# A hybrid attention and convolution layer: half of the conv gate by Strassen, adaLN columns moved, norm1's operands in pieces, norm2's statistics one unit later

## The chip, the cores and the metric

One core of one Trainium2 chip runs the kernel. The metric is the device time of one execution in microseconds (us), as the median of several runs. TensorE is called PE, VectorE DVE, ScalarE ACT, GpSimd POOL; SP is the queue from which the transfers here are issued.

## The reference

One layer of an encoder, 1024 prompt tokens and 32 sample tokens (T = 1056 columns), width 1024, all in float32:

```python
mod = (jax.nn.silu(c) @ w_ada + b_ada).reshape(B, 6, 1, D_MODEL)
shift1, scale1, gate1, shift2, scale2, gate2 = [mod[:, i] for i in range(6)]
h = _rms_norm(x, norm1_g) * (1 + scale1) + shift1
q, k, v, xin, gb, gc, ga_br, gb_br = jnp.split(h @ w_in, IN_SPLITS, axis=-1)
...
y_a = o.reshape(B, T, ATTN_DIM) @ w_attn_out          # o: differential attention of q, k, v
u = gc * xin
cv, conv_tail = _short_conv(u, conv_prev, conv_w)     # three taps along time
y_b = (gb * cv) @ w_conv_out
m = jax.nn.sigmoid(ga_br) * y_a + jax.nn.sigmoid(gb_br) * y_b
x = x + gate1 * (m @ w_out)
h2 = _rms_norm(x, norm2_g) * (1 + scale2) + shift2
g, up = jnp.split(h2 @ w_gate_up, 2, axis=-1)
x = x + gate2 * ((jax.nn.silu(g) * up) @ w_down)
```

## The kernel before

Channels lie on the 128 partitions, tokens on the free axis. A float32 operand is split into a high part (an ACT cast) and a low part (a DVE subtraction, L83 to L85), and a product is three matmuls: high by high, high by low, low by high. There are two forms. The classical one takes a column chunk of 128 output channels in three groups of 352 tokens: 8 tiles of the input width, 3 products, 3 groups, 72 matmuls of 352 columns (L1047 to L1049 in the attention, L1075 to L1077 after it). The Strassen form (`wstrassen`, `strassen`, matmul at L181) takes a pair of chunks at once: seven products instead of eight, on quarters of 264 tokens in two groups g of two quarters each, 7 × 2 × 12 = 168 matmuls of 264 columns. Its combining adds are DVE's (L188 to L197).

The stages follow each other. **Start**: columns of `w_ada` are loaded (`ada_load`) and multiplied (`ada_matmul`, `ada_close`, L330 to L345), x is normalised and transposed (`x_norm`, `x_transpose`), modulated (`modulate`), and its Strassen operands are formed (`h_operands(j, g)`, on DVE and ACT, four j by two groups). **Conv loop**: for pairs p = 0, 2, 4, 6 a Strassen call for xin (section 3 of `w_in`) and one for gc (section 5), the multiply u (L474) and the convolution on DVE (L503, L505), whose result goes to `cv_d` in DRAM. **Gate calls**: eight Strassen calls for sections 6 and 7, and behind each two `ada_step`: one column of the remaining 32 (sections 2, 4, 3, 5) per step, computed on DVE (`ada_dve`: 2 instructions of L354, 14 of L357) and, a step later, summed over partitions by two PE transposes into a PSUM tile called pad (L364) and a DVE reduction (L366). Then the eight tiles of h come back from DRAM (`hA`, L567).

**Attention**: 72 units (8 heads, 9 query tiles) whose order a planner writes out, with priorities and estimated durations. Section 4 of `w_in` (gb, times the convolution's result, into `z_d`) is computed there as `filler`: eight classical chunks, in 192 steps that the planner puts where PE has nothing else; what is left follows the last unit. **Conv projection** (`first_w`, `zt`, the loop over n, L1075 to L1094): the first two column chunks run tile by tile as the eight z tiles come in through two staging buffers and are split; the other six run by token groups, one `ada_step` behind each. **Attention projection**: eight column chunks with an `ada_step` each, and then the steps that are left. **Output projection** with the residual (`out_unit`): the last four chunks by quarters q = 0, 2, 1, 3. The squares of the new x are summed on DVE (L1205), `stat(q)` sums them over partitions on PE (L1213) and takes the power on POOL (L1216), and norm2's operands for the Strassen form of gate and up follow (`spread` L1224, `h2_block` L1230 and L1234). A table `after` says behind which unit (q, i) each of these steps stands. **Gate and up** by Strassen, then **down**.

Each engine works in its own order. Outside the attention a scheduler sets it from the order of the code and its own estimates.

## Time and profile before

| | us |
|---|---|
| median of 3 runs | 2137.67 (2137.27 to 2138.59) |
| the profiled execution | 2132.99 |
| span in its trace | 2131.2 |
| PE busy | 2031.0 |
| DVE busy | 1351.4 |
| ACT busy | 847.1 |
| POOL busy | 364.7 |

The trace counts from the start of the span. A row of the timeline gives the start, the duration, the engine, the line and operation, the tile written and those read, the shape, and in brackets the idle time of the engine before it with what ended it. A line number is that of the kernel before.

### The profile page before, as it was taken

What the parts mean: (1) busy time and instruction counts of PE and PEld (TensorE: products, weight loads), DVE (VectorE), ACT (ScalarE), POOL (GpSimd) and SP (SyncE); (2) the same over time, 40 slices, a digit from 0 to 9 for tenths busy, and PEclk for the clock granted to TensorE, in tenths of its full rate; (3) what the DMA queues carried; (4) which work ended last, traced back from release to release, by engine and by line L of the source; (5) the groups of instructions that cost most, each with busy time, mean ns of one, the idle gap of its engine ahead of it and who ended that gap; (6) DMA issues with size and microseconds to landing.
All of it is one profiled execution on the core that took longest, in us unless ns stands there. A gap on an engine that the chain in (4) does not pass through costs nothing. (4 is left out here: it accounts for less than half of the span.)

```text
span 2131.2 us, 37806 instructions
## 1 busy us (share of the span) xinstructions
PE 2031.0 (95%) x14339; PEld 1976.7 (93%) x14339; DVE 1351.4 (63%) x3096; ACT 847.1 (40%) x2044; POOL 364.7 (17%) x660
## 2 busy tenths in 40 slices
PE   7799999899999999999899989889999999999999
PEld 5799999899999999999899989879999999989998
DVE  4988799967766776677357974685555555432322
ACT  5522233366666666666222213463332332321210
POOL 1023100033333333333000000012112112100000
PEclk8899999999999999999999999999999999999999
DMA  8422254532211221121388625123222222552321
GB/s 251 151 84 90 71 161 135 192 89 60 68 57 56 62 59 54 50 69 48 114 258 250 198 90 170 53 68 122 71 73 89 70 80 79 172 157 65 99 69 57
DMA packets 298960, 224.42 MB, mean 105 GB/s; under 512 B 15617, under 2 KB 281498, under 8 KB 298778
## 3 DMA queue, kind: packets, MB, share of 16 engines
q1 hardware_dynamic: 298778, 222.00, 34.0%
q8 instruction: 113, 1.85, 0.4%
q14 instruction: 69, 0.57, 0.1%
HBM read 162.46 MB, written 59.49 MB: 104 GB/s over the span
## 5 line engine op out<-in xcount | busy, mean ns | idle before, releaser
L84 ACT CAST ws<-st 128x512 fp32r<-128x512 f32 x360 | 217.2, 615 | 564.4 <-PE u L181 172.9
L181 PE MATMUL u<-op,ws 128*128 128x264 f32 x3168 | 397.3, 285 | 7.8 <-ACT op L84 6.5
L181 PEld LDWEIGHTS u<-op,ws 128*128 128x128 f32 x3168 | 392.4, 189 | 8.4 <-ACT op L84 6.7
L85 DVE TENSOR_TENSOR ws<-st,ws 128x512 fp32r<-128x512 f32 (+1 forms) x322 | 222.6, 699 | 195.3 <-ACT ws L84 192.9
L181 PE MATMUL u<-T,ws 128*128 128x264 f32 x1536 | 198.5, 287 | 1.2 <-DVE sg L197 1.2
L181 PEld LDWEIGHTS u<-T,ws 128*128 128x128 f32 x1536 | 193.5, 190 | 1.8 <-DVE sg L197 1.8
L731 PE MATMUL b<-qw,hA 128*128 128x384 f32 x512 | 186.8, 365 | 2.5 <-DVE adred L366 1.2
L732 PE MATMUL b<-qw,hA 128*128 128x384 f32 x512 | 174.2, 340 | 0.6 <-DVE qw L688 0.6
L733 PE MATMUL b<-qw,hA 128*128 128x384 f32 x512 | 173.8, 339 | 0.0
L1431 PE MATMUL u<-ka,ws 128*128 128x352 f32 x480 | 156.8, 327 | 4.6 <-ACT ka L84 2.8
L1432 PE MATMUL u<-ka,ws 128*128 128x352 f32 x480 | 155.6, 324 | 2.3 <-DVE ka L85 2.3
L181 PE MATMUL u<-B,ws 128*128 128x264 f32 x1152 | 152.1, 287 | 4.6 <-ACT B L84 4.6
L1433 PE MATMUL u<-ka,ws 128*128 128x352 f32 x480 | 155.7, 324 | 0.0
L181 PEld LDWEIGHTS u<-B,ws 128*128 128x128 f32 x1152 | 145.6, 190 | 5.3 <-ACT B L84 4.9
L357 DVE SCALAR_TENSOR_TENSOR adacc<-adw,sc,adacc 128x128 f32<-128x128 f32 x448 | 132.8, 350 | 0.6
L879 ACT ACTIVATE p<-S,nmx,rs 128x128 f32<-128x128 f32 (+5 forms) x144 | 113.1, 787 | 50.1 <-DVE nmx L959 17.0
L85 POOL TENSOR_TENSOR ws<-st,ws 128x512 fp32r<-128x512 f32 x38 | 49.8, 1311 | 445.3 <-ACT ws L84 426.1
L731 PEld LDWEIGHTS b<-qw,hA 128*128 128x128 f32 x512 | 97.7, 191 | 6.4 <-issue 2.1
L732 PEld LDWEIGHTS b<-qw,hA 128*128 128x128 f32 x512 | 97.9, 191 | 1.2 <-DVE qw L688 0.9
L733 PEld LDWEIGHTS b<-qw,hA 128*128 128x128 f32 x512 | 97.2, 190 | 0.0
L1431 PEld LDWEIGHTS u<-ka,ws 128*128 128x128 f32 x480 | 90.6, 189 | 5.6 <-ACT ka L84 3.5
L1432 PEld LDWEIGHTS u<-ka,ws 128*128 128x128 f32 x480 | 90.7, 189 | 3.1 <-DVE ka L85 3.1
(277 smaller groups left out, 4379.8 us busy)
## 6 DMA issues: line engine op xcount, KB each, us to landing
adw<-in_w_ada_dram SPq DMA_DIRECT2D x48, 512.0 KB, 4.0
st<-in_w_gate_up_dram SPq DMA_DIRECT2D x44, 512.0 KB, 4.0
st<-in_w_in_dram SPq DMA_DIRECT2D x43, 512.0 KB, 4.3
sa<-a_d SPq DMA_DIRECT2D x22, 528.0 KB, 3.6
a_d<-xa SPq DMA_DIRECT2D x84, 132.0 KB, 1.7
st<-in_w_in_dram SPq DMA_DIRECT2D x42, 256.0 KB, 2.9
st<-in_w_down_dram SPq DMA_DIRECT2D x16, 512.0 KB, 5.0
h_d<-xnT SPq DMA_DIRECT2D x8, 528.0 KB, 4.3
```

Source lines behind the costliest of these rows:

```text
L84: act.copy(hi, src)
L85: (lo_eng or dve).tensor_sub(lo, src, f(hi))
L181: pe.matmul(q[dst], l, t[:, r, j, :], start=first and j == n == 0, stop=j == 3 and n == 2, skip_group_check=not first)
L357: dve.scalar_tensor_tensor(out=acc[:, s_, :], in0=st[:, kt, :], scalar=sc[:, 8 * s_ + kt:8 * s_ + kt + 1], in1=acc[:, s_, :], op0=ALU.mult ...
L731: pe.matmul(pj[:, 0:384], a, qh[:, :, c, :], start=kt == 0, stop=False)
L732: pe.matmul(pj[:, 0:384], a, ql[:, :, c, :], start=False, stop=False)
L733: pe.matmul(pj[:, 0:384], b, qh[:, :, c, :], start=False, stop=kt == KT - 1)
L879: act.activation(p[:n, :u["L"]], u["sv"][m][:n], AF.Exp, bias=u["nmx"][:n, m:m + 1], scale=u["rs_t"][:n, m:m + 1], accum_out=sums[:n, m:m ...
L1431: pe.matmul(pt[:, :gw], wh, ah, start=kt == 0, stop=False)
L1432: pe.matmul(pt[:, :gw], wh, al, start=False, stop=False)
L1433: pe.matmul(pt[:, :gw], wl, ah, start=False, stop=kt == KC - 1)
```

## The change

1. In the conv loop, for p = 0 and p = 2, section 4 is now a Strassen call too (`conv_out`), behind the convolution. Its result is multiplied by the convolution's in place, on DVE for the first quarter of each group and on POOL for the other three, and goes to `z_d`; these two pairs no longer go through `cv_d`. `filler` takes only the chunks n = 4 to 7.
2. The last gate call has no `ada_step` behind it; in the conv projection n = 2 to 5 have two. The steps behind the attention projection's loop are none.
3. At the start `ada_order`'s loads and x's loads are interleaved, and the multiplications by columns of `w_ada` (`ada_two`) stand between x's tiles. `h_operands(j, k)` forms group 0 alone, j = 0 and 1 together, and through a tile `hs`. Group 1 is formed by `h_operands_rest`, in pieces over all four j at once, in place in xnT; a hook takes one piece after each of the seven steps of the first Strassen call, under a PE and DVE order as written.
4. `stat(0)`, `stat(2)` and `stat(1)` stand one unit later.

```diff
+    hs = E.tile([P, 2, T], F32, tag="sg", name="hs", bufs=1)
-    def h_operands(j, g):
+    def h_operands(j, k):
...
+    def h_operands_rest():
+
+        def parts(o, src):
+            split(src, Top[o, 1][:, 0], Top[o, 1][:, 1])
+
+        b11, b12, b21, b22 = (xnT[:, 4 * i:4 * i + 4, q * QW:(q + 1) * QW] for i in (0, 1) for q in (1, 3))
+        parts("B11", b11)
+        dve.tensor_sub(b11, b12, b11)
+        yield
+        parts("T1", b11)
+        yield
...
     for j in range(4):
+        if j > 1:
+            ada_two()
+            ada_two()
+            ada_close()
+        modulate(j)
+        modulate(j + 4)
         if j:
-            for i in range(4):
-                ada_matmul()
-                if 7 + 4 * j + i < len(ada_order):
-                    ada_load(ada_order[7 + 4 * j + i])
-            ada_close()
+            h_operands(0 if j == 1 else j, j + 1)
         if j == 2:
             w0 = wstrassen(win_pair(3, 0))
-        modulate(j)
-        modulate(j + 4)
-        h_operands(j, 0)
-        if j:
-            h_operands(j - 1, 1)
     for n in range(KT):
         sp.dma_start(h_d[n], xnT[:, n, :])
-    h_operands(3, 1)
+    rest = h_operands_rest()
...
+    def conv_out(w, p, z):
+        def epi(i, j, g, src):
+            c0 = (g + 2 * j) * QW
+            zb = z[:, i, c0:c0 + QW]
+            (dve if i == j == 0 else pool).tensor_mul(zb, src, zb)
+            sp.dma_start(z_d[p + i, :, c0:c0 + QW], zb)
+
+        strassen(w, (0, 1), lambda i, j, g: tmp("t"), epi)
+
+    NZ = 4
...
-            conv_in(w0, p, (0,), xin)
+            with tc.manual_schedule(engines={mybir.EngineType.PE, mybir.EngineType.DVE}):
+                conv_in(w0, p, (0,), xin, lambda k, g: next(rest))
...
+        if p < NZ:
+            w = wstrassen(win_pair(4, p))
         z = V.tile([P, 2, T], F32, tag="z", name="z", bufs=1)
...
-            sp.dma_start(cv_d[p + i], z[:, i])
+            if p >= NZ:
+                sp.dma_start(cv_d[p + i], z[:, i])
+        if p < NZ:
+            conv_out(w, p, z)
...
-            ada_step()
-            ada_step()
+            if (sec, p) != (7, KT - 2):
+                ada_step()
+                ada_step()
...
-        for n in range(KT):
+        for n in range(NZ, KT):
...
-        ada_step()
+        for _ in range(2 if n < KT - 2 else 1):
+            ada_step()
...
-    after = {(2, 0): lambda: stat(0), (2, 2): lambda: first(0, 0), (1, 0): lambda: stat(2), (1, 2): g0_second,
-             (3, 0): lambda: stat(1), (3, 2): g1_first}
+    after = {(2, 1): lambda: stat(0), (2, 2): lambda: first(0, 0), (1, 1): lambda: stat(2), (1, 2): g0_second,
+             (3, 1): lambda: stat(1), (3, 2): g1_first}
```

The order of instructions shows the moves at three places. First PE, between the last gate call and the first projections of the attention. Before:

```order
L181 MATMUL u<-B_388,ws 128x264 x12
L181 MATMUL u<-T_389,ws 128x264 x12
L181 MATMUL u<-T_390,ws 128x264 x12
L364 MATMUL pad<-ident,adacc 128x128 x6
L731 MATMUL b<-qw,hA 128x384
L732 MATMUL b<-qw,hA 128x384
L733 MATMUL b<-qw,hA 128x384
```

and with the change (L790 to L792 are the lines L731 to L733):

```order
L181 MATMUL u<-B_450,ws 128x264 x12
L181 MATMUL u<-T_451,ws 128x264 x12
L181 MATMUL u<-T_452,ws 128x264 x12
L364 MATMUL pad<-ident,adacc 128x128 x2
L790 MATMUL b<-qw,hA 128x384
L791 MATMUL b<-qw,hA 128x384
L792 MATMUL b<-qw,hA 128x384
```

Four of the six pads have left this place; the last two columns are summed elsewhere.

Second PE, at the end of the attention: the last two transposes of the units (into b, from on), and the filler (b from hA and wf). Before:

```order
L821 MATMUL b_13367<-ident_83,on_13362 128x128
L1047 MATMUL b_13311<-hA_5108,wf_12945 128x352
L1048 MATMUL b_13311<-hA_5108,wf_12945 128x352
L1049 MATMUL b_13311<-hA_5108,wf_12946 128x352
L1047 MATMUL b_13311<-hA_5113,wf_12945 128x352
L1048 MATMUL b_13311<-hA_5113,wf_12945 128x352
L1049 MATMUL b_13311<-hA_5113,wf_12946 128x352
L821 MATMUL b_13391<-ident_83,on_13389 128x32
L1047 MATMUL b_13402<-hA_5078,wf_13396 128x352
L1048 MATMUL b_13402<-hA_5078,wf_13396 128x352
L1049 MATMUL b_13402<-hA_5078,wf_13397 128x352
L1047 MATMUL b_13402<-hA_5083,wf_13396 128x352
```

and with the change, from the last unit's transposes of p to the first matmuls of the conv projection (u from z and ws; L862, L873 and L880 are the lines L803, L814 and L821):

```order
L862 MATMUL b_13613<-ident_83,p_13598 128x32
L862 MATMUL b_13613<-ident_83,p_13598 32x32
L873 MATMUL b_13621<-V_12393,aT_13616 32x128 x2
L880 MATMUL b_13624<-ident_83,on_13619 128x128
L880 MATMUL b_13638<-ident_83,on_13636 128x32
L1134 MATMUL u_13712<-z_13674,ws_13658 128x352
L1135 MATMUL u_13712<-z_13674,ws_13658 128x352
L1136 MATMUL u_13712<-z_13674,ws_13658 128x352
```

The filler's steps between and behind the last units are gone from here, and the conv projection stands right behind the last transpose.

Third DVE, from the last column chunk of the attention projection (m, sg) to the first residual of the output projection (xa). Before:

```order
L1131 TENSOR_TENSOR m_15555<-m_15555,sg 128x352
L367 TENSOR_SCALAR mod<-adred,vec 128x2
L354 TENSOR_SCALAR adacc<-adw,sc 128x128 x2
L357 SCALAR_TENSOR_TENSOR adacc<-adw,sc,adacc 128x128
L85 TENSOR_TENSOR m<-m_15555,m 128x352
L357 SCALAR_TENSOR_TENSOR adacc<-adw,sc,adacc 128x128 x12
L366 TENSOR_REDUCE adred<-pad 128x2
L357 SCALAR_TENSOR_TENSOR adacc<-adw,sc,adacc 128x128
L367 TENSOR_SCALAR mod<-adred,vec 128x2
L354 TENSOR_SCALAR adacc<-adw,sc 128x128 x2
L357 SCALAR_TENSOR_TENSOR adacc<-adw,sc,adacc 128x128 x14
L366 TENSOR_REDUCE adred<-pad 128x2
```

and with the change (L1190, L1191 and L1229 are the lines L1130, L1131 and L1169):

```order
L357 SCALAR_TENSOR_TENSOR adacc<-adw,sc,adacc 128x128 x3
L1190 TENSOR_TENSOR sg<-u,sg 128x352
L1191 TENSOR_TENSOR m_15627<-m_15627,sg 128x352
L85 TENSOR_TENSOR m<-m_15627,m 128x352
L1190 TENSOR_TENSOR sg<-u,sg 128x352
L366 TENSOR_REDUCE adred<-pad 128x2
L1191 TENSOR_TENSOR m_15627<-m_15627,sg 128x352
L367 TENSOR_SCALAR mod<-adred,vec 128x2
L366 TENSOR_REDUCE adred<-pad 128x2
L85 TENSOR_TENSOR m<-m_15627,m 128x352
L367 TENSOR_SCALAR mod<-adred,vec 128x2
L1229 COPY xa<-x 128x512
```

The runs of 13 and 14 multiply-adds behind the last m are gone; the last column's are now ahead of it.

## Rows read from the trace of the kernel before

**Rows 1.** The page: the busy time of PE and PEld and the other engines with their shares; and the granted clock by slice of a fortieth of the span.

```profile
PE 2031.0 (95%) x14339; PEld 1976.7 (93%) x14339; DVE 1351.4 (63%) x3096; ACT 847.1 (40%) x2044; POOL 364.7 (17%) x660
...
PEclk8899999999999999999999999999999999999999
```

**Rows 2.** The table of PE's waits: line, what it waited for, and the sum, number and longest in us.

```profile
PE pad L364 <- DVE adacc L357: 17.2, 5, 7.4
...
PE x L342 <- ACT adarow L335: 7.3, 2, 5.0
...
PE x L1213 <- DVE ssq L1205: 6.2, 3, 4.5
...
PE u L181 <- ACT B L84: 4.6, 1, 4.6
```

**Rows 3.** The timeline of PE, at the first product of a Strassen call in the gate-and-up stage, and of the call that follows it.

```profile
1441.64 0.53 PE L181 MATMUL u<-op,ws 128*128 128x264 f32 x3
...
1462.22 0.41 PE L181 MATMUL u<-op,ws 128*128 128x264 f32 x2
```

**Rows 4.** The table of stretches: the stretch, its length, busy time (and number of instructions) of PE, PEld, DVE, ACT and POOL, the granted clock, DMA share and GB/s. The conv stage of p = 0; the second and third call in it; the last units; the filler behind them; the first two and then another column chunk of the conv projection.

```profile
99.40:162.00 62.60, 61.67 (x504) 61.46 (x503) 53.74 (x116) 15.28 (x29) 17.09 (x26) 1.00 0.29 86
120.00:141.70 21.70, 20.77 (x170) 20.56 (x169) 21.13 (x43) 5.36 (x11) 7.13 (x12) 1.00 0.40 126
141.70:162.00 20.30, 20.30 (x168) 20.30 (x167) 13.91 (x28) 5.01 (x9) 5.71 (x8) 1.00 0.18 53
1002.00:1027.00 25.00, 22.32 (x148) 19.48 (x147) 15.68 (x39) 13.85 (x43) 5.09 (x13) 1.00 0.16 49
1027.00:1067.70 40.70, 37.15 (x216) 36.25 (x217) 11.93 (x17) 6.43 (x8) 0.00 (x0) 0.96 0.43 137
1067.70:1094.70 27.00, 24.48 (x146) 23.01 (x144) 15.85 (x36) 7.68 (x9) 0.00 (x0) 1.00 0.83 255
1130.80:1142.70 11.90, 11.90 (x77) 11.86 (x76) 7.66 (x23) 2.23 (x3) 0.00 (x0) 1.00 0.89 264
```

**Rows 5.** Groups by line and shape (busy us, mean ns of one, idle before): POOL's multiply of 264 columns from 99 to 400 us; DVE's two-input operation of 264 columns from 60 to 100 us, and from 99 to 162 us.

```profile
L474 POOL TENSOR_TENSOR u<-t,sg 128x264 f32<-128x264 f32 x16 | 18.2, 1138 | 54.9 <-DVE t L197 54.9
...
L197 DVE TENSOR_TENSOR sg<-u,u 128x264 f32<-128x264 f32 x4 | 1.7, 428 | 0.0
...
L188 DVE TENSOR_TENSOR u<-u,p 128x264 f32<-128x264 f32 x6 | 2.5, 425 | 0.0
```

**Rows 6.** Line 1047, the first of the filler's three products (a step has one): from 1001 to 1027 us (number, duration min/median/max, first and last start), and in the groups of 1027 to 1067.7 us.

```profile
L1047 PE MATMUL b<-hA,wf x24: 321/330/431, 1001.8 to 1023.8; 128*128 128x352 f32 x24
...
L1047 PE MATMUL b<-hA,wf 128*128 128x352 f32 x72 | 24.1, 334 | 1.3 <-ACT wf L1033 1.3
```

**Rows 7.** The timeline of PE and ACT from the last unit to the third column chunk of the conv projection.

```profile
1025.53 0.21 PE L821 MATMUL b<-ident,on 32*128 32x32 f32 x1 [1.05 <-DVE on L986]
1027.05 0.43 PE L1047 MATMUL b<-hA,wf 128*128 128x352 f32 x1 [1.31 <-ACT wf L1033]
...
1064.53 1.07 ACT L84 CAST z<-st 128x1056 fp32r<-128x1056 f32 x1 [3.25 <-PE b L1049]
...
1067.56 0.32 PE L1049 MATMUL b<-hA,wf 128*128 128x352 f32 x1
1067.72 0.33 PE L1075 MATMUL u<-z,ws 128*128 128x352 f32 x1
...
1094.74 0.40 PE L1075 MATMUL u<-z,ws 128*128 128x352 f32 x1 [0.54 <-DVE sg L1094]
```

**Rows 8.** A group of 1067.7 to 1094.7 us: ACT's casts of the z tiles.

```profile
L84 ACT CAST z<-st 128x1056 fp32r<-128x1056 f32 x6 | 6.4, 1075 | 16.2 <-DMA st<-z_d 16.2
```

**Rows 9.** The timeline around the attention's start, PE first, then DVE and ACT.

```profile
421.94 0.44 PE L364 MATMUL pad<-ident,adacc 128*128 128x128 f32 x1 [7.44 <-DVE adacc L357]
...
424.83 0.66 PE L731 MATMUL b<-qw,hA 128*128 128x384 f32 x1 [1.25 <-DVE adred L366]
...
419.35 2.71 DVE L357 SCALAR_TENSOR_TENSOR adacc<-adw,sc,adacc 128x128 f32<-128x128 f32 x10
...
441.95 1.05 ACT L1033 CAST wf<-st 128x1024 fp32r<-128x1024 f32 x1 [5.38 <-DMA st<-in_w_in_dram]
```

**Rows 10.** Groups on DVE from 1118.5 to 1166 us: the multiply-adds of the adaLN columns.

```profile
L357 DVE SCALAR_TENSOR_TENSOR adacc<-adw,sc,adacc 128x128 f32<-128x128 f32 x45 | 13.2, 348 | 0.0
```

**Rows 11.** The timeline of PE at the end of the attention projection.

```profile
1260.64 0.60 PE L364 MATMUL pad<-ident,adacc 128*128 128x128 f32 x4
...
1271.48 0.64 PE L1075 MATMUL u<-m,ws 128*128 128x352 f32 x1
...
1272.21 0.49 PE L1077 MATMUL u<-m,ws 128*128 128x352 f32 x1
1272.50 0.49 PE L1075 MATMUL u<-m,ws 128*128 128x352 f32 x1
```

**Rows 12.** The timeline of norm2's statistics, DVE and then PE.

```profile
1372.36 1.25 DVE L1258 TENSOR_TENSOR h<-h,h 128x1056 f32<-128x1056 f32 x1
...
1374.10 1.41 PE L1213 MATMUL x<-ones,ssq 128*128 128x1 f32 x6 [4.49 <-DVE ssq L1205]
...
1409.07 0.59 PE L181 MATMUL u<-op,ws 128*128 128x264 f32 x1 [6.48 <-ACT op L84]
```

**Rows 13.** The stretch of the first Strassen call, with columns as in rows 4.

```profile
70.30:99.40 29.10, 24.46 (x169) 23.86 (x169) 26.57 (x79) 17.30 (x39) 0.44 (x4) 0.79 0.34 104
```

More of the change, by code (lines that the diff above doesn't have):

```diff
@@ L386, in modulate @@
         dve.tensor_scalar(out=y, in0=y, scalar1=a1[:, n, 1:2], scalar2=mod[:, n, 1:2], op0=ALU.mult, op1=ALU.add)
-    def h_operands(j, g):
+    hs = E.tile([P, 2, T], F32, tag="sg", name="hs", bufs=1)
+    def h_operands(j, k):
         def parts(o, src):
-            t = Top[o, g]
-            split(src, t[:, 0, j, :], t[:, 1, j, :])
-        b11, b12 = (xnT[:, j, q * QW:(q + 1) * QW] for q in (g, g + 2))
-        b21, b22 = (xnT[:, j + 4, q * QW:(q + 1) * QW] for q in (g, g + 2))
-        t1, t2, t3 = (X0.tile([P, QW], F32, tag=f"t{i}", name="ht", bufs=1) for i in (1, 2, 1))
+            t = Top[o, 0]
+            split(src, t[:, 0, j:k, :], t[:, 1, j:k, :])
+        b11, b12 = (xnT[:, j:k, q * QW:(q + 1) * QW] for q in (0, 2))
+        b21, b22 = (xnT[:, j + 4:k + 4, q * QW:(q + 1) * QW] for q in (0, 2))
+        t1, t2, t3 = (hs[:, i, :(k - j) * QW].rearrange("p (a b) -> p a b", b=QW) for i in (0, 1, 0))
         parts("B11", b11)
@@ L407, in h_operands @@
         parts("T4", t2)
+    def h_operands_rest():
[7 more added lines that the diff above has]
+        yield
+        dve.tensor_sub(b11, b22, b11)
+        parts("T2", b11)
+        yield
+        parts("B21", b21)
+        dve.tensor_sub(b12, b22, b12)
+        yield
+        parts("T3", b12)
+        yield
+        parts("B22", b22)
+        yield
+        dve.tensor_sub(b21, b21, b11)
+        parts("T4", b21)
+        yield
     ada_order = [sec * KT + n for j in range(4) for n in (j, j + 4) for sec in (0, 1)]
@@ L412, in hybrid_layer, with ada_two @@
     load_rows()
-    for i in range(9):
+    for i in range(4):
         x_load(i)
-    for c in ada_order[4:7]:
+    for c in ada_order[4:6]:
         ada_load(c)
-    for c in ada_order[7:11]:
-        ada_matmul()
-        ada_load(c)
+    for i in range(4, 9):
+        x_load(i)
+    ada_load(ada_order[6])
+    late = list(ada_order[7:])
+    def ada_two():
+        for _ in range(2):
+            ada_matmul()
+            if late:
+                ada_load(late.pop(0))
+    ada_two()
+    ada_two()
     rows_to_vec()
     ada_close()
-    for i in range(9):
+    for i in range(4):
         x_norm(i)
-        if i % 4 == 3:
-            x_transpose(range(i - 3, i + 1), range(KT))
+    x_transpose(range(0, 4), range(0, 4))
+    ada_two()
+    x_transpose(range(0, 4), range(4, KT))
+    for i in range(4, 9):
+        x_norm(i)
+    x_transpose(range(4, 8), range(0, 4))
+    ada_two()
+    x_transpose(range(4, 8), range(4, KT))
+    ada_close()
     x_transpose((8,), range(KT))
@@ L430, in hybrid_layer @@
     for j in range(4):
[L431 to L436 removed]
+        if j > 1:
+            ada_two()
+            ada_two()
+            ada_close()
+        modulate(j)
+        modulate(j + 4)
+        if j:
+            h_operands(0 if j == 1 else j, j + 1)
         if j == 2:
             w0 = wstrassen(win_pair(3, 0))
[L439 to L443 removed]
     for n in range(KT):
         sp.dma_start(h_d[n], xnT[:, n, :])
[L446 removed]
+    rest = h_operands_rest()
     attention_constants()
@@ L458, in segs, with conv_in @@
         return ([(c0, c1, c0 + 2)] if c1 <= S else [(c0, S, c0 + 2), (S, c1, S + 4)])
-    def conv_in(w, p, gs, xin):
+    def conv_in(w, p, gs, xin, hook=None):
         def dest(i, j, g):
@@ L466, in epi @@
                 act.copy(dest(0, 0, g), src)
-        strassen(w, gs, dest, epi)
+        strassen(w, gs, dest, epi, hook)
     def conv_gate(w, p, u, xin):
```

1 line of the change is left out of this document (removed).

## The prediction

> **What bounds the kernel now.** I read the page first: TensorE (PE) is busy for 95% of the span and its granted clock is at full nearly everywhere [rows 1]. So the time is the matmul columns plus the places where PE waits or runs at the lower of its two clock levels. The table of PE's waits comes second and gives the places: the pads of the modulation on VectorE, 17.2 us in five waits; the waits at the start (7.3 and 4.6); the squares' sums of norm2 (6.2) [rows 2]. The third view is the table of stretches, which says what the neighbours do there. The fourth, the timeline, gives the steps of the sum. A reader should see that each edit aims at one of these places except the Strassen one, which works on the columns themselves.
>
> I sum against the profiled execution (2132.99 us, span 2131.2) and carry the difference to the median of the runs, 2137.67, which stands 4.68 above it.
>
> **Strassen for half of the filler: the added side.** One Strassen call is 168 matmuls of 264 columns; from 1441.64 to 1462.22 one takes 20.6 us [rows 3]. Two calls are added, after the gate calls of p=0 and p=2: +41.1 us on PE, which has nothing else there to hide them behind. VectorE is the neighbour to fear. Over the conv stretch from 99.40 to 162.00 it is busy 53.74 of 62.60 us, and 21.13 of 21.70 in the call where the convolution lies [rows 4]; PE loses 0.9 us there. The new call brings another 13.9 us or so of VectorE work in 20.6 (that is what the call at 141.70 has [rows 4]), so the pair as a whole stays under PE's time. GpSimd gets six multiplies of 264 columns a pair at 1.14 us [rows 5], and is idle for three quarters of that stretch. Bounds for the two calls: 41.1 with no wait, 45 with two waits of about 1 us in each; I take 42, near the row where PE lost 0.9.
>
> One rule of the Trainium skill speaks against this edit. "SBUF — State Buffer", in its terms, says that VectorE and GpSimd arbitrate for one shared pair of ports, and that the loser blocks for a whole instruction. By it the twelve multiplies would block VectorE for 13.7 us, by an estimate from the GpSimd row. The trace does not bear this out in the durations: VectorE's two-input form of 264 columns takes 0.43 us both before 99 us, where GpSimd hardly works, and after it, where it does [rows 5]. By the rule the sum would be some 1 to 2 us higher, inside the bound.
>
> **The removed side.** Four of eight classical column chunks go, 288 matmuls of 352 columns. At the steady 0.16 us [rows 7] that is 46.4 us of PE. The order shows where: the first 96 of the 192 steps stay in the attention; of those that go, 24 lie among the last units, and 72 make the block from 1027.05 to 1067.72, three chunks with nothing else on PE [rows 6, 7]. The block's 40.7 us lie on the path. The 24 steps among the units (11.6 us) were cover: PE was busy 22.32 of 25.0 us there [rows 4], and the last units then wait on their own chain of softmax, transpose and normalisation, whose last PE step stands at 1025.53 [rows 7]. I credit nothing for those 24; between 0 and 4 us could come of a chain that no longer queues behind filler, or be lost if the thin stretch runs at 1.2 GHz.
>
> What is late next? The conv projection's first two columns run through z tile by tile. In the old order z0 was cast at 1064.53, because it queued behind the filler, and the 144 matmuls from 1067.72 to 1094.74 took 27.0 us where 23.2 would do: ScalarE waited 16.2 us for z to land, at a DMA share of 0.83 [rows 4, 7, 8]. In the new kernel all of z_d is written before the last units, but its first load still comes after the first two weight columns' loads, through the two staging buffers, and their splits stand behind the last units' work on ScalarE and VectorE. So I let the block start about 2.5 us after the last unit (1028) and last the same 27 us: the third column starts at 1055.5 where it started at 1094.74. That is −39 us; bounds −42 (z fully ahead, 23.2 us) and −33 (units slower, load late). Conv and filler together thus come to only +3: the Strassen saving (5.3 us) is spent in the uncovered tail.
>
> **Two modulation columns fewer at the end of the gate calls.** Behind the last gate call PE waits 7.44 us until 421.94 for VectorE's sums of columns 15 and 16, and 1.25 us more before the first projection at 424.83 [rows 9]. In the new order two pads stand there, and VectorE takes the h tiles at once, without the 2.71 us run of sums at 419.35 and its like; the last h tile would come some 4 us earlier. But the first key and query work waits for ScalarE, which at 441.95 stands behind a filler weight's DMA that starts by the stage buffers' turn [rows 9]. I take −4.5, bounds −8 (the whole wait goes) and −1 (the DMA holds).
>
> **The same columns in the conv projection.** n=2..5 get two each. One costs VectorE 2 multiplies and 14 multiply-adds of 0.348 us [rows 10]; ten in a row take 2.71 us, since they overlap [rows 9], so 16 take 16 × 0.27 = 4.3. Of 11.9 us a column VectorE was busy 7.66 with one in it [rows 4]; with 4.3 more, 12.0. So it is just full, and another load of weights comes on top of a DMA share of 0.89 [rows 4]. Six PSUM tiles, two columns, stand between PE and VectorE and soak up a short lag. +1.5, bounds 0 and +7.
>
> **The end of the attention projection.** Its last matmuls end at 1260.64; then PE waits behind the last columns' sums, the bulk of the 17.2 us of pads [rows 2], and resumes at 1271.48, the matmuls first spaced 0.29 instead of 0.16 us [rows 11]. All of that is trailing work which the new order does not have: four pads remain, whose sums lie inside the projection. What is late next is m of the last column, which the first output unit needs only at its eighth tile, 3.4 us in. −10.8 of waiting, −1.2 for some ten matmuls at the half clock, +0.6 left over for four pads: −11.4, bounds −12 and −8.
>
> **norm2's statistics one unit later.** PE waits 4.49 us at 1374.10 for the squares' sum [rows 12]. The sum is late because VectorE does h blocks of 1.25 us ahead of it. A unit of 24 matmuls of 264 columns (2.9 us) now stands before each: of 6.2 us in three waits [rows 2] that covers 2.9 of the longest and all of the other two, 4.6 us. But VectorE is nearly without pause there, and the 6.48 us at 1409.07 [rows 12] waits for ScalarE's and VectorE's operands and not for the statistics: time gained early is partly waited later. −4, bounds −8 (that wait shrinks too) and 0 (all of it waited later).
>
> **The start.** Group 0's operands come first, two pieces merged; group 1 in pieces of 1056 columns between the steps of the first call, which takes 29.1 us instead of 20.6 [rows 3], the wait of 4.6 and a granted clock of 0.79 among it [rows 2, 13]. VectorE is 26.57 of 29.10 us busy in it [rows 13], and that is what the pieces relieve: a two-input operation takes 1.25 us at 1056 columns [rows 12] and 4 × 0.43 at 264 [rows 5], so group 1's eleven cost 5.2 us less. I count a third of it, since the call also waits for loads and for the modulation before it: −1.6, bounds −6 and +3 (a hook's piece standing ahead of a combining add, so PE waits for PSUM).
>
> **Sum.** +42 − 39 − 4.5 + 1.5 − 11.4 − 4 − 1.6 = −17.0: 2116.0 in the profiled execution's terms, 2120.7 in those of the median.
>
> **Rivals.**
> The clock stays low (slower). Without filler PE has thin work from about 1003 and a hole of some 2.5 us at 1026. If the z block and the column behind it ran at 1.2 GHz, 216 matmuls would take 0.29 instead of 0.16 us [rows 11]: +28, less the 3.8 that z's landing hides, +24, so about 2145. It decides from some 195 matmuls at the lower level. Against it: after the 1.31 us hole at 1027.05 [rows 7] the granted clock of the next 40.7 us was still 0.96 [rows 4]. The Trainium skill, "TensorE: Matmul & The Clock Gate" (HAM oscillation), tells of a kernel in which every wait for data dropped the clock anew; by it each z wait would re-arm the loss. The trace speaks against it: the waits in the z block of before left the clock at 1.00.
> VectorE becomes the bound at the new places (less gain). Attention start and norm2 give nothing, wco costs 5, the conv calls 3 more: 2120.7 + 4.5 + 4 + 3.5 + 3 = 2136, within 0.2%.
> The waits vanish wholly (more gain): start −6, attention −8, norm2 −8: about 2109.
> That the change doesn't do what it says is settled by the order, save for its start.
>
> **Chances.** My sum with its neighbours down to 2108 and up to 2130: 0.76; more gain than that: 0.06; VectorE-bound, around 2136: 0.11; clock low or another wait of that size: 0.07. The range is 2106 to 2135, half of the VectorE-bound case in it. This kernel's measurement can tell about 0.2%, so faster is below 2133.4 and slower above 2141.9: faster 0.84, same 0.10, slower 0.06.
>
> **What would show it.** In the profile after: pads on VectorE gone from the head of PE's waits; two calls of 20.6 to 22 us in the conv stage; last unit to first conv-projection matmul 1.5 to 4 us, and 24 to 28 us for the z block; line 1094's columns at 12.0 to 13 us; out stage right behind the projection; the statistics' wait under 2 us. A z block above 35 us at a granted clock of 0.5, or conv calls above 24 us, would make the forecast wrong.

## The result and the profile after

The changed kernel takes 2142.61 us (median of 10 runs, 2139.5 to 2149.6), the kernel before 2137.06 (10 runs, 2131.48 to 2138.72): ratio 1.0032, 95% interval 1.0020 to 1.0045 (the two medians alone give 1.0026). It is slower by 0.3%, where 17 us less had been forecast. The profiled execution took 2139.57 us, its span is 2137.8, 6.6 more than before; I explain these 6.6.

The table gives the start of PE's work at the same place in both traces, and how far the changed kernel lags there. Where the lag changes from a line to the next, time went or came. The Strassen calls are counted from the start: the third is the added one of section 4 in the changed kernel, and the xin call of p = 2 in the kernel before; in both it runs beside the convolution on VectorE.

| PE's first instruction of | before | after | lag |
|---|---|---|---|
| the first Strassen call | 70.29 | 73.12 | +2.8 |
| the second call | 99.44 | 106.58 | +7.1 |
| the third call | 120.00 | 127.14 | +7.1 |
| the fourth call | 141.75 | 152.26 | +10.5 |
| the last gate call | 393.02 | 444.14 | +51.1 |
| the first transpose of queries (L756) | 446.07 | 491.70 | +45.6 |
| the last transpose of the last unit (L821) | 1025.53 | 1071.73 | +46.2 |
| the conv projection's third column chunk | 1094.74 | 1101.94 | +7.2 |
| the attention projection | 1166.38 | 1181.59 | +15.2 |
| the output projection | 1271.48 | 1278.28 | +6.8 |
| gate and up, first call | 1386.89 | 1386.01 | −0.9 |
| gate and up, second call | 1421.09 | 1427.93 | +6.8 |

The page after, the lines that answer to [rows 1]: engine busy times as there, and the granted clock by slice.

```profile
PE 2034.9 (95%) x14387; PEld 1979.0 (93%) x14387; DVE 1362.9 (64%) x3080; ACT 850.4 (40%) x2030; POOL 376.1 (18%) x674
...
PEclk8899999999999999999999999989999999999999
```

PE is as full as before. One slice more shows an 8, the one from 1390 us, in which the first gate-and-up call waits (below).

PE's waits after, in answer to [rows 2]:

```profile
PE u L181 <- ACT op L84: 6.5, 1, 6.5
PE u L1134 <- ACT ws L84: 6.2, 1, 6.2
...
PE u L181 <- DVE sg L197: 4.5, 1, 4.5
PE b L790 <- ACT V L915: 4.3, 1, 4.3
...
PE u L181 <- ACT ws L84: 2.9, 1, 2.9
...
PE u L181 <- DVE ws L85: 2.3, 1, 2.3
```

The pads fall from 17.2 us to 0.3 and the squares' sums from 6.2 to 1.6. New ones stand in their place: 6.2 us for the first weights of the attention projection, 4.5 for a combining add at the start, and weights of the first gate-and-up call (2.9 and 2.3). The 6.5 us on the last operand is as it was.

**Start.** The first call on PE, in answer to [rows 13], and below it VectorE in the middle of it:

```profile
73.10:106.60 33.50, 24.92 (x170) 24.05 (x171) 26.00 (x48) 16.33 (x26) 1.96 (x5) 0.85 0.25 80
```

```profile
86.60 1.73 PE L181 MATMUL u<-B,ws 128*128 128x264 f32 x12 [1.63 <-DVE w L191]
92.84 3.01 PE L181 MATMUL u<-T,ws 128*128 128x264 f32 x12 [4.52 <-DVE sg L197]
...
88.85 1.26 DVE L85 TENSOR_TENSOR T<-xnT,T 128x1056 fp32r<-128x1056 f32 x1 [1.14 <-ACT T L84]
90.03 1.25 DVE L85 TENSOR_TENSOR B<-xnT,B 128x1056 fp32r<-128x1056 f32 x1
91.20 1.25 DVE L426 TENSOR_TENSOR xnT<-xnT 128x1056 f32<-128x1056 f32 x1
92.36 0.43 DVE L197 TENSOR_TENSOR sg<-u,w 128x264 f32<-128x264 f32 x1
```

PE stands for 4.52 us before the product at 92.84. What it waits for is the combining add L197 at 92.36 (0.43 us), and on VectorE that stands behind three pieces of 1.25 us in a row. VectorE is not short of time in this call: it is busy for 26.00 of 33.50 us, where it was 26.57 of 29.10 [rows 13], and before the low part of three of its pieces it waits 1.83, 1.14 and 0.80 us for ScalarE's cast of the same piece. The 2.8 us by which the first call starts later are not explained; in runs whose start is that of before it lies anywhere from 68.56 (e13) to 72.63 (e10).

**Conv projection.** Four stretches of 12 us after, columns as in [rows 4]: the fifth and sixth column chunk, the last two with two modulation columns, then the seventh and eighth. Below, the loads on SP's queue and ScalarE's casts that lead to the attention projection at 1181.59, and under them the first load of its weights in the trace before:

```profile
1126.50:1138.50 12.00, 12.00 (x78) 11.96 (x78) 11.62 (x43) 2.22 (x3) 0.00 (x0) 1.00 0.92 282
1138.50:1150.60 12.10, 12.10 (x79) 11.96 (x78) 12.10 (x42) 2.23 (x3) 0.00 (x0) 1.00 0.75 227
1150.60:1162.60 12.00, 12.00 (x75) 11.74 (x75) 12.00 (x40) 1.14 (x2) 0.00 (x0) 1.00 0.75 220
1162.60:1174.70 12.10, 11.69 (x74) 11.38 (x73) 8.52 (x26) 1.44 (x2) 0.00 (x0) 1.00 0.84 276
```

```profile
1160.71 0.38 SPq L1146 DMA_DIRECT2D st<-oT_d  x1
...
1167.95 0.64 SPq L1146 DMA_DIRECT2D st<-oT_d  x1
...
1176.73 0.38 SPq L107 DMA_DIRECT2D st<-in_w_attn_out_dram  x1
...
1166.05 1.07 ACT L84 CAST o<-st 128x1056 fp32r<-128x1056 f32 x1 [4.15 <-DMA st<-oT_d]
1174.33 1.08 ACT L84 CAST o<-st 128x1056 fp32r<-128x1056 f32 x1 [7.21 <-DMA st<-oT_d]
...
1180.92 1.14 ACT L84 CAST ws<-st 128x512 fp32r<-128x512 f32 x2 [3.20 <-DVE adacc L357]
```

```profile
1158.07 0.38 SPq L107 DMA_DIRECT2D st<-in_w_attn_out_dram  x1
```

VectorE is full in the sixth and seventh (12.10 of 12.10, 12.00 of 12.00). The o tiles' casts wait for their loads until 1166.05 and 1174.33, the staging buffers come free late, and the first weights of the attention projection are asked for only at 1176.73 (1158.07 before). From the third column chunk to the last matmul of the stage it takes 1.5 us more than before; the other 6.5 us of the lag come behind it, with the wait of 6.2.

**Statistics.** PE at the first gate-and-up call, in answer to [rows 12]:

```profile
1386.01 1.63 PE L181 MATMUL u<-op,ws 128*128 128x264 f32 x12
1390.54 0.63 PE L181 MATMUL u<-op,ws 128*128 128x264 f32 x2 [2.90 <-ACT ws L84]
1393.50 2.57 PE L181 MATMUL u<-op,ws 128*128 128x264 f32 x10 [2.33 <-DVE ws L85]
1395.87 1.27 PE L1273 MATMUL x<-ones,ssq 128*128 128x1 f32 x6
...
1401.80 0.73 PE L1284 MATMUL x<-ident,rs 128*128 128x128 f32 x6
...
1415.06 0.59 PE L181 MATMUL u<-op,ws 128*128 128x264 f32 x1 [6.50 <-ACT op L84]
```

The call's first product starts 0.9 us earlier than before. Its second waits 2.90 and 2.33 us for weights, and the fourth statistic (L1273) and its spread (L1284) stand on PE behind that; the last operand comes at 1415.06, where it came at 1409.07.

**Attention's end.** The stretch from the last 25 us of the units to the first z product, and the z block:

```profile
1047.00:1073.40 26.40, 15.40 (x74) 12.56 (x74) 16.23 (x40) 15.19 (x44) 5.30 (x13) 0.74 0.17 50
1073.40:1101.90 28.50, 26.68 (x144) 25.75 (x145) 19.91 (x44) 8.36 (x9) 0.00 (x0) 0.88 0.85 266
```

The granted clock is 0.74 in the thin stretch, as feared in the slow rival, but the lag of the attention grows by only 0.6 us over its units. The z block's start, and a place in the z block of e1 (below), right behind a wait of 1.66 us for z:

```profile
1073.40:1080.00 6.60, 5.97 (x19) 5.59 (x20) 3.09 (x3) 2.15 (x2) 0.00 (x0) 0.50 0.66 209
```

```profile
1092.90:1097.30 4.40, 4.39 (x18) 4.39 (x19) 2.00 (x4) 0.00 (x0) 0.00 (x0) 0.61 0.88 259
```

So the block does begin at the lower level, 0.50, with matmuls 0.29 us apart; from 1080.00 to 1101.90 the granted clock is 1.00. Some 19 matmuls at 0.29 instead of 0.16 us are an estimated 2.5 us, and PE's waits in the block are 1.8 us where they were 2.6: it lasts 28.6 us instead of 27.0.

### The profile page after: what moved, and what is told of

Its sections match the earlier page's. It is cut to its first block, busy times and chain, and to the rows that moved or that the text cites. A ratio compares the mean times of both kernels' runs of the same rounds, so it can differ in the third digit from the quotient of the medians.

```text
span 2137.8 us, 37879 instructions
## 1 busy us (share of the span) xinstructions
PE 2034.9 (95%) x14387; PEld 1979.0 (93%) x14387; DVE 1362.9 (64%) x3080; ACT 850.4 (40%) x2030; POOL 376.1 (18%) x674
## 5 line engine op out<-in xcount | busy, mean ns | idle before, releaser
L84 ACT CAST ws<-st 128x512 fp32r<-128x512 f32 x374 | 226.4, 615 | 583.4 <-PE u L181 180.5
L181 PE MATMUL u<-op,ws 128*128 128x264 f32 x3168 | 401.4, 287 | 13.3 <-ACT op L84 6.5
L181 PEld LDWEIGHTS u<-op,ws 128*128 128x128 f32 x3168 | 395.9, 190 | 14.4 <-ACT op L84 6.7
L85 DVE TENSOR_TENSOR ws<-st,ws 128x512 fp32r<-128x512 f32 (+1 forms) x334 | 231.8, 701 | 200.5 <-ACT ws L84 198.3
L181 PE MATMUL u<-T,ws 128*128 128x264 f32 x1728 | 224.6, 288 | 7.1 <-DVE sg L197 4.5
L181 PEld LDWEIGHTS u<-T,ws 128*128 128x128 f32 x1728 | 219.0, 191 | 7.7 <-DVE sg L197 4.7
L790 PE MATMUL b<-qw,hA 128*128 128x384 f32 x512 | 186.4, 364 | 6.9 <-ACT V L915 4.3
L181 PE MATMUL u<-B,ws 128*128 128x264 f32 x1296 | 170.4, 287 | 4.1 <-ACT B L84 2.4
L792 PE MATMUL b<-qw,hA 128*128 128x384 f32 x512 | 173.4, 339 | 0.7 <-DVE hA L85 0.7
L181 PEld LDWEIGHTS u<-B,ws 128*128 128x128 f32 x1296 | 163.6, 189 | 4.7 <-ACT B L84 2.6
L85 POOL TENSOR_TENSOR ws<-st,ws 128x512 fp32r<-128x512 f32 x40 | 52.9, 1322 | 457.0 <-ACT ws L84 439.0
L790 PEld LDWEIGHTS b<-qw,hA 128*128 128x128 f32 x512 | 97.1, 190 | 11.2 <-ACT V L915 4.6
L792 PEld LDWEIGHTS b<-qw,hA 128*128 128x128 f32 x512 | 96.7, 189 | 1.3 <-DVE hA L85 1.3
```

Of the source, the lines that this page charges most:

```text
L84: act.copy(hi, src)
L85: (lo_eng or dve).tensor_sub(lo, src, f(hi))
L181: pe.matmul(q[dst], l, t[:, r, j, :], start=first and j == n == 0, stop=j == 3 and n == 2, skip_group_check=not first)
L790: pe.matmul(pj[:, 0:384], a, qh[:, :, c, :], start=kt == 0, stop=False)
L792: pe.matmul(pj[:, 0:384], b, qh[:, :, c, :], start=False, stop=kt == KT - 1)
```

## The experiments

Ratios are against the kernel before, run beside each on the same chip. "Before" stood between 2134.99 and 2136.94 us in the four sets. The first four do one part of the change each.

**e1_conv_only**

```diff
+        if p < NZ:
+            w = wstrassen(win_pair(4, p))
...
+        if p < NZ:
+            conv_out(w, p, z)
...
-        for n in range(KT):
+        for n in range(NZ, KT):
```

NZ is 4, as in the change.

> Only the Strassen call for half of section 4 (two calls in the conv loop, a filler of four chunks). Theory (each part has its own price, read from the trace after): two calls cost 41.1 us and 3 to 4 more in the call behind the convolution of p=0, the tail of the attention gives back 38 to 39, so +3 to +7 us against before. Rival (the parts act alone as forecast and disturb one another only together): +3 us, with the conv calls at 20.6 us each and no wait in them.

2140.02 us, ratio 1.0020 (1.0011 to 1.0028), +4.4. In its trace the second call lags by 1.1 us and the last gate call by 42.1, so that the two calls cost 40.9; the third column chunk of the conv projection lags by 5.4. The call beside the convolution takes 22.1 us (25.1 in the change), so that loss belongs to another part. The size is within the theory's range, and the interval reaches the rival's +3; that no such wait is there speaks for the rival.

**e2_ada_only**

```diff
-            ada_step()
-            ada_step()
+            if (sec, p) != (7, KT - 2):
+                ada_step()
+                ada_step()
...
-        ada_step()
+        for _ in range(2 if n < KT - 2 else 1):
+            ada_step()
```

> Only the modulation columns moved from the last gate call and from behind the attention projection into the conv projection. Theory: about -5 us: -4.6 at the attention's start, -11 to -12 at the end of the attention projection, but +8 to +11 in the conv projection, most of it one wait of PE for the first weights of the attention projection, whose load stands on SP behind loads of w_ada columns that wait for a free buffer. Rival (forecast): -14.4 us, with the conv projection's columns at 12.0 to 12.6 us and no such wait.

2135.43 us, ratio 0.9997 (0.9988 to 1.0005): nothing. The attention starts 4.0 us earlier and the attention projection, up to the output projection, gives 8.5, but from the conv projection's fourth column chunk to the attention projection it takes 70.8 us instead of 58.9 (the expectations of the later runs call that chunk the third). Of this PE waits 6.9 us in one piece for the first weights of the attention projection, as expected:

```profile
1175.02 0.66 PE L1076 MATMUL u<-o,ws 128*128 128x352 f32 x1 [6.91 <-ACT ws L84]
```

The forecast's −14.4 falls; so does my own −5, by the size of the loss.

**e3_start_only**: operands, hook and order of loads as in the change, all else as before.

```diff
         if j:
...
+            h_operands(0 if j == 1 else j, j + 1)
...
-        h_operands(j, 0)
-        if j:
-            h_operands(j - 1, 1)
...
+    rest = h_operands_rest()
...
+                conv_in(w0, p, (0,), xin, lambda k, g: next(rest))
```

> Only the start: order of loads, group 0 of norm1's operands first, group 1 in pieces in the first Strassen call. Theory: +6 to +9 us, because group 1's operands are all left to VectorE inside the first call, in a written order where the combining adds stand behind pieces of 1.25 us; the second call starts at 106 us instead of 99. Rival (forecast): -1.6 us, the second call at 98 us.

2146.82 us, ratio 1.0051 (1.0039 to 1.0063), +11.2: more than I expected. The second call lags by 8.9 us, and the fourth by 12.3: the loss in the third call is this part's.

**e4_stats_only**

```diff
-    after = {(2, 0): lambda: stat(0), ... (1, 0): lambda: stat(2), ... (3, 0): lambda: stat(1), ...
+    after = {(2, 1): lambda: stat(0), ... (1, 1): lambda: stat(2), ... (3, 1): lambda: stat(1), ...
```

> Only norm2's statistics one unit later. Theory: -1 to +1 us: the waits of PE at the statistics shrink by about 4 us, but the last quarter's operands, on ScalarE and VectorE, are ready no earlier, so the wait in the first gate-and-up call grows by as much. Rival (forecast): -4 us, with the wait before the second product of the last operands unchanged at 6.5 us.

2138.34 us, ratio 1.0013 (1.0004 to 1.0021): slower by 2.7, outside both. The first gate-and-up call starts 6.4 us earlier than before, the second 2.8 later.

The parts' sum is 4.4 − 0.2 + 11.2 + 2.7 = 18, the whole change 5.5. They are not additive: at the output projection's start the lags in the single traces are +4.3 (e1), +0.2 (e2) and +10.7 (e3), 15.2 together, where the whole change has 6.8. That the losses of one part are covered by waits of another is likely, but which by which is not shown. The next runs take the parts' mechanisms.

**e5_ada_three_buffers**: as e2, with three buffers for a column of `w_ada` (nb is 3 in the conv projection).

```diff
-        st = sbp.tile([P, KT, P], F32, tag="adw", name="adw", bufs=2)
+        st = sbp.tile([P, KT, P], F32, tag="adw", name="adw", bufs=nb)
```

> As e2_ada_only, with three buffers instead of two for a column of w_ada in the conv projection, so that its load on SP waits less for VectorE and holds up less behind it. Theory (the loads behind it on SP are held up): the conv projection's last columns and the first weights of the attention projection come earlier; the 11.9 us that e2 loses between its third column chunk and the attention projection shrinks to 6 or less, and the kernel is 4 to 8 us faster than before. Rival (VectorE is full, and the splits and the sums on it set the pace): the 11.9 us stays within 2 us.

2135.05 us, ratio 0.9998 (0.9988 to 1.0007); 70.5 us between the fourth column chunk and the attention projection. The theory of the held-up loads gets nothing from this.

**e6_start_loads** and **e7_start_pieces** halve e3. e6 has the order of loads and multiplications and forms the operands by (j, g) as before; e7 has the diff of e3 alone. The edit of e6:

```diff
-    for i in range(9):
+    for i in range(4):
         x_load(i)
...
         if j:
-            for i in range(4):
-                ada_matmul()
...
+        if j > 1:
+            ada_two()
+            ada_two()
```

> Of the start's change only the order of loads and of the modulation's multiplications; the operands of both groups are formed as before. Theory (two causes in e3: the first call starts 3.7 us later because of the order of loads and multiplications, and takes 5.2 us longer because of the deferred pieces): first call starts 2 to 4 us later, and takes its 29 us; +2 to +4 us in all. Rival (all of e3's loss is the pieces): 0.

2134.85 us, ratio 0.9998 (0.9988 to 1.0009): nothing.

> Of the start's change only the operands: group 0 first, group 1 in pieces inside the first call; loads and multiplications in the order of before. Theory: the first call starts within 1 us of before, takes some 34 us instead of 29, and the call behind the convolution loses 3 us more: +6 to +9 us. Rival (the loss is the loads'): 0 to -2 us.

2147.27 us, ratio 1.0050 (1.0036 to 1.0065). The rival of e6 is right: all of e3's loss is the pieces (+12.3 here, +11.2 there). The first call takes 34.3 us instead of 29.2.

**e8_last_columns_late**: no `ada_step` in the last gate call, one each in the conv projection as before, none behind the attention projection; the last four columns go into gate and up.

```diff
-    while ada_todo or ada_open:
-        ada_step()
+    while ada_open:
+        ada_open.pop(0)()
...
         gate_up(f0, 1, (0, 1), sblk)(w)
+        if f0 >= 4 and ada_todo:
+            ada_open.append(ada_halves(*ada_todo.pop(0), PSB, "x", Z))
```

> The kernel before, but with the last gate call's two modulation columns and the two behind the attention projection (four in all, of gate2, which only the last stage reads) moved into the gate-and-up stage, where VectorE is busy for about half of the time; their loads come in two halves. Nothing is added to the conv projection. Theory (the two waits of part 2 can be had without a cost where VectorE and SP have room): -4 at the attention's start and -10 to -11 at the end of the attention projection, nothing back: 2119 to 2124 us against 2136 of before. Rival (what follows is late anyway and takes the gain back, as in the statistics): -5 us or less.

2119.00 us, ratio 0.9926 (0.9913 to 0.9938), −16.0. The timeline of PE at the end of the attention projection, the place of [rows 11]:

```profile
1255.42 0.32 PE L1104 MATMUL u<-o,ws 128*128 128x352 f32 x1
1255.58 0.60 PE L364 MATMUL pad<-ident,adacc 128*128 128x128 f32 x4
1255.94 0.41 PE L1102 MATMUL u<-m,ws 128*128 128x352 f32 x1
```

From the pads to the next matmul it took 10.8 us before [rows 11], and takes 0.36 here. In gate and up VectorE's busy time rises from 241.35 to 263.62 of 432 us, and PE stays at 432.00.

**e9_extra_sums_no_loads** and **e10_extra_loads_no_sums** take e2's four extra columns apart. For the second column of a pair (`extra[0]`) e9 reads the tile of the column before (NOLOAD), e10 leaves out the multiply-adds (NOSUM):

```diff
+        if extra[0] and NOLOAD:
+            st = last[-1]
...
-            for kt in range(1, KT):
+            for kt in range(1, 1 if extra[0] and NOSUM else KT):
```

> As e2_ada_only, but the four columns that the conv projection has more than before are not loaded: their sums on VectorE read the tile of the column before, so gate2 and the columns behind it come out of other data; no arithmetic is left out. Theory (the four loads, on SP's queue and the DMA engines, push the o tiles and the first weights back): the time between the conv projection's third column chunk and the attention projection falls from 70.8 us to 60 to 63 us, and the kernel is 8 to 11 us faster than before. Rival (the sums on VectorE do it): 69 to 71 us, and the kernel's time is that of before.

(The four columns are one of norm2's scale and three of its shift, not gate2's.) 2133.35 us, ratio 0.9986 (0.9974 to 0.9997), −2.2; 72.8 us between the two places.

> As e2_ada_only, but of the sums of the four columns more only the two first multiplies of each are left (2 of 16 instructions), with all loads: their modulation comes out incomplete. Theory (the loads do it): 67 to 71 us between the third column chunk and the attention projection, and the kernel's time is within 4 us of before. Rival (the sums on VectorE do it): 60 to 62 us, and 9 to 11 us faster than before.

2124.54 us, ratio 0.9943 (0.9928 to 0.9958); 63.3 us. My theory of the loads falls, the rival holds in the main: the sums on VectorE do most of it, and 4.4 us of the 11.9 stay (the rival had 60 to 62 us). PE's wait for the first weights of the attention projection is 6.9 us in e2, 8.3 in e5 and 4.6 in e9; in e10 there is none. The stretch between the two places in e2 and in e10, columns as in [rows 4]:

```profile
1104.20:1175.00 70.80, 60.86 (x379) 59.47 (x376) 59.53 (x185) 12.74 (x17) 0.00 (x0) 0.98 0.83 255
```

```profile
1104.00:1167.30 63.30, 60.33 (x378) 59.50 (x377) 47.77 (x139) 13.25 (x17) 0.00 (x0) 1.00 0.90 275
```

With the sums VectorE is busy for 59.53 of 70.80 us, without them for 47.77 of 63.30, at a DMA share of 0.90.

**e11_pieces_behind**

```diff
-                conv_in(w0, p, (0,), xin, lambda k, g: next(rest))
+                conv_in(w0, p, (0,), xin)
+                list(rest)
```

> As e7_start_pieces, but group 1's pieces stand behind all of group 0's combining adds instead of between them. Theory (the loss is the deferral: pieces over all four j cannot begin before the last modulation, and VectorE has all of group 1 to do from then on, wherever the pieces stand): the second call starts at 104 to 110 us, as in e7 or later, against 99.4 before; the waits on combining adds (6.8 and 1.6 us) go and waits for group 1's operands come. Rival (the loss is the order, pieces ahead of combining adds): the second call at 98 to 101 us.

2142.35 us, ratio 1.0031 (1.0019 to 1.0044). The second call starts at 107.65, no earlier than e7's 105.67, and PE's waits in the first call change their names. From e7 and then from e11, up to 110 us:

```profile
PE u L181 <- DVE sg L197: 4.5, 1, 4.5
...
PE u L181 <- ACT B L84: 2.4, 1, 2.4
...
PE u L181 <- DVE w L191: 1.6, 1, 1.6
```

```profile
PE u L181 <- ACT T L84: 4.9, 1, 4.9
...
PE u L181 <- ACT B L84: 2.4, 1, 2.4
...
PE u L181 <- DVE B L85: 1.6, 1, 1.6
...
PE u L181 <- DVE T L85: 0.9, 1, 0.9
```

The order has a share: e11 does not have e7's loss in the third call (21.7 us, e7 25.5), and is 5 us faster. The other 6.8 us stay. That they are the deferral's is not shown by this run: in its written order VectorE may not touch a piece before group 0's last add, and idles 6.5 us between the adds from 79.11 to 87.01. No run changes the width of the pieces alone, or frees their order alone.

**e12_stat3_one_product_earlier**, on e4:

```diff
-                if k == 1:
+                if k == 0:
                     stat(3)
-                if k == 3:
+                if k == 2:
                     g1_third()
```

> As e4_stats_only, with the fourth statistic and the step that reads it one product earlier in the first gate-and-up call. Theory (e4 loses because the fourth statistic stands on PE behind two products whose weights are split late, 3.4 and 2.6 us of waits): 2 to 5 us faster than e4, 0 to 3 us faster than before. Rival (ScalarE's and VectorE's work on the last quarter sets the end, whenever its statistic comes): within 1 us of e4.

2135.20 us, ratio 0.9999 (0.9988 to 1.0009), 3.1 below e4 (another set). The spread (L1224) moves from 1397.26 in e4 to 1395.72; PE still waits 2.45 us for weights, and 5.76 for the last operand, at 1409.96. This points to the place of the fourth statistic, behind late weights, as e4's loss; the gain forecast is not there even then.

**e13_conv_one_pair** is e1 with one pair; **e14_late_one_pair** and **e15_late_two_pairs** are e8 with e13 and with e1.

```diff
-    NZ = 4
+    NZ = 2
```

> As e1_conv_only, but by Strassen only for p=0: one call of 20.6 us more, and a filler of six chunks, of which 24 of 144 steps still lie among the last units and 24 behind them. Theory (e1 loses because its filler ends before the last units, so that they and the z tiles' landing lie open): the saving of columns comes through, 20.6 us added and 23.2 us of the block behind the last unit gone, with the same 27 us from the first z tile to the third column chunk: -2 to -3 us against before. Rival (the added call costs more than its columns wherever it stands): 0 to +2 us.

2129.76 us, ratio 0.9967 (0.9955 to 0.9979), −7.2: better than expected. It has one call more than before and a filler that outlasts the units. The stretches of the last units, of the 24 steps behind them, and of the z block:

```profile
1016.00:1042.80 26.80, 25.38 (x170) 22.44 (x169) 18.24 (x45) 13.43 (x41) 6.70 (x16) 1.00 0.17 50
1042.80:1059.10 16.30, 14.68 (x73) 14.12 (x74) 6.68 (x9) 5.49 (x8) 0.00 (x0) 0.79 0.49 156
1059.10:1083.90 24.80, 23.67 (x147) 23.09 (x145) 15.83 (x37) 7.16 (x8) 0.00 (x0) 1.00 0.89 275
```

PE is busy 25.38 of 26.80 us among the units, at full clock, where the change had 15.40 of 26.40 at 0.74; the z block, whose first tiles land behind the filler, takes 24.8 us.

> e8_last_columns_late with one Strassen pair as in e13. Theory (the two are independent): -2 to -3 us against e8, 2116 to 2117 us. Rival (the one takes back part of the other): the time of e8 or more.

2116.39 us, ratio 0.9902 (0.9887 to 0.9916): the fastest here, 20.6 us below before.

> e8_last_columns_late with two Strassen pairs as in the change. Theory: the 4 us of e1 are lost here too: 2122 to 2125 us, and 6 to 8 us slower than e14. Rival (the two pairs cost nothing once the modulation columns are out of the way): the time of e14 within 2 us.

2121.39 us, ratio 0.9934 (0.9917 to 0.9952): 5.0 slower than one pair, a little less than expected.

## Why the prediction was wrong, point by point

| term | forecast | in the trace after |
|---|---|---|
| start, up to the second call; and the third call | −1.6 | +7.1; +3.4 |
| two conv calls, up to the last gate call | +42 | +40.6 |
| two columns fewer at the attention's start | −4.5 | −5.5 |
| filler, up to the third column chunk | −39 | −38.4 |
| conv projection with two columns each | +1.5 | +8.0 |
| end of the attention projection | −11.4 | −8.4 |
| norm2's statistics, up to the second gate-and-up call | −4 | 0.0 |
| what follows | 0 | −0.2 |
| sum | −17.0 | +6.6 |

**Right.** The Strassen part and the attention's start, in mechanism and size: columns are saved, the uncovered tail eats the saving. e1 and e13 show the tail's share: with the filler kept past the last unit one pair gains 7.2 us, with two pairs and no filler 4.4 are lost. At the attention's start the first projection comes 11.0 us sooner after the last gate call, and 4.3 are waited later for ScalarE (the line of L790 and V above), as the forecast had feared. Of the signs that the prediction names, the pads, the columns at 12.0 to 12.5 us, the output stage right behind the projection and the statistics' wait came as said. The first of the added calls did not: it took 25.1 us, above the 24 that would make the forecast wrong, and by e1 and e3 that loss is the start's. No sign lay in the first call, at the first weights of the attention projection or in the first gate-and-up call, where the rest was lost.

**The slow rival** comes nearest in time (2145) by luck. It needs some 195 matmuls at the lower level; the z block has about 19 of them, and took 1.6 us more and not 24. The rule of the Trainium skill, "TensorE: Matmul & The Clock Gate" (HAM oscillation), that a wait drops the clock anew is borne out in part: in e1 a wait of 1.66 us is followed by a stretch at 0.61, while waits of 0.87 and 0.32 us in the z block after left it at full.

**The start: the step that failed is "that is what the pieces relieve".** I counted VectorE's instructions, 5.2 us fewer, and gave a third. I did not ask when they can begin. A piece over all four j needs the last modulated tile; the old form did part of group 1 before the first call, between the modulations. Of the 88 operand operations of 264 columns, 45 stood before the first call in the trace before and as much as 33 of them do now, none of group 1. So VectorE's busy time in the call fell by 0.6 us and not by 5.2, its pieces alternate with ScalarE's casts, and PE waits 8.6 us in the call where it waited 4.6. e7 shows this part alone to cost 12.3 us, e6 the loads nothing, e11 that moving the pieces behind the adds gives back 5 of them. The bound (+3, a piece ahead of a combining add) named a true mechanism, at less than those 5. How the rest divides between the deferral, the width of the pieces and the fixed order stays open.

**The conv projection: the step that failed is "just full" as a price of +1.5.** 12.0 of 11.9 us was worked out rightly (12.10 of 12.10 measured), and inside the stage the loss is the +1.5 of the forecast. But the sum has nothing for what VectorE's lag holds up behind the stage, and that is 6.5 us. VectorE splits the o tiles too; these leave the two staging buffers late, and the first weights of the attention projection queue for the same buffers. e10 shows that the sums do most of it, e5 that a third buffer for the column's weights doesn't help, e9 that leaving out the loads hardly does. The chain from a late split over the staging buffer to the weights is read from the trace, not tried alone.

**The end of the projection** gave what was forecast at its place (−10.5 from its fifth column chunk on), less 2.1 that the first column chunk takes longer: behind the 6.2 us wait the granted clock is 0.60 up to 1187 us.

**The statistics: the step that failed is the bound of zero on one side.** I wrote that time gained would partly be waited later; all of it was, and e4 lost more. An earlier first product found its weights unsplit, and on PE the fourth statistic stood behind that product. e12 takes it out of there and is even with before. What the forecast had wrong is the path: the last operand follows the spread of the fourth statistic by 13.3 to 14.2 us in all four traces (before, after, e4, e12), and the change does not move that statistic. Its spread stands 124.2 us behind the output projection's start before, 123.5 after, 127.2 in e4 and 123.2 in e12. What fills those 13 us, ScalarE's modulations (13 of them take 5.25 us from 1403.86 on) or the splits, stays open.

**VectorE as the bound** (2136) had the right engine at two of its four places: norm2 gave nothing and the conv projection cost 8.0 (it said 5). The attention's start and the conv calls came as in the forecast, and for the start it had the forecast's −1.6.

**The shared port pair.** The rule of the Trainium skill ("SBUF — State Buffer", Terms), that the loser blocks, is borne out by the trace, and the prediction's reading against it was wrong: it took a form that has one input in PSUM. The low part of a split (L85) reads both inputs from SBUF; from e1, in the added call beside the convolution, VectorE and below it GpSimd's multiplies:

```profile
139.13 0.68 DVE L85 TENSOR_TENSOR ws<-st,ws 128x512 fp32r<-128x512 f32 x1
...
140.41 1.12 DVE L85 TENSOR_TENSOR ws<-st,ws 128x512 fp32r<-128x512 f32 x1
...
140.23 1.91 POOL L483 TENSOR_TENSOR z<-t,z 128x264 f32<-128x264 f32 x2 [6.99 <-DVE t L197]
```

Four such splits stand under the twelve multiplies, each longer by 0.43 us. PE loses nothing by it: the two calls take 40.9 us, for 41.1 forecast without a wait.

## What to carry to other kernels

Work that is moved to an engine with room still has a first moment at which it can start and a last one at which it is needed; count it there, not over the stage. An engine that is "just full" can hold up what frees a buffer, and the price shows behind the stage: here 1.5 us inside it and 6.5 at the next stage's first weights. Look for a stage after the one that is full: the four modulation columns cost nothing where their reader is far away and VectorE is busy for just over half of the time, and gained 16 us. A filler was worth keeping here where a chain without cover stood behind it, even though its columns could be had cheaper elsewhere.

## What the runs showed that I had not expected

The parts alone add up to +18 us, together they make +5.5. One Strassen pair gains 7.2 us where its columns are worth 2.6. In its trace the z tiles land behind the filler, and the z block falls from 27.0 to 24.8; from the last unit to the z block it takes 16.4 us where it took 42.2, 25.8 less for columns worth 23.2. Why is not shown. A VectorE operation with both inputs in SBUF took 1.12 us instead of 0.68 under a GpSimd multiply. The kernel before spreads over 7 us from run to run (2131.48 to 2138.72); with ten runs of each kernel the interval is still 2.7 us to either side.
